# Holding the small products of the head norms behind a turning of attention weights

## The chip, the core and the metric

The kernel runs on one core of one Trainium2 chip. It is one launch that takes all inputs from the chip's memory and writes the whole result back. The metric is the device time of that launch in microseconds (us). TensorE (PE in the profile) multiplies matrices and writes into PSUM, eight banks of 128 partitions by 512 float32 values. VectorE (DVE) and ScalarE (ACT) read those banks. GpSimd (POOL) and SyncE (SP) only issue transfers during the stretch that matters here. Each engine works through a queue of its own in a fixed order, and an instruction at the head of a queue that waits for another engine holds everything behind it.

## The reference

The reference is a trunk of two layers over 512 tokens of width 1024: attention with its output projection, a gated feed-forward part, a short convolution, and another feed-forward part, each with a residual sum and a norm. Only the attention layer is touched. It has 16 heads of 64 values. Eight of them are forgetting heads (softmax with a decay), eight are stick-breaking heads. Queries and keys are normed per head before their products are taken:

```python
q_fox = rms_norm(q[:, :H_FOX], fox_q_g)
k_fox = rms_norm(k[:, :H_FOX], fox_k_g)
q_sb = rms_norm(q[:, H_FOX:], sb_q_g)
k_sb = rms_norm(k[:, H_FOX:], sb_k_g)
...
logits = jnp.einsum('bhqd,bhkd->bhqk', qi, k)
...
return jnp.einsum('bhqk,bhkd->bhqd', w, v)
```

For the stick-breaking heads the weights `w` come from two sigmoids and a running product over the keys; for the forgetting heads they are a softmax. Both are causal, in blocks of 128 queries.

## The kernel before, in words

The heads are worked off in eight pairs, p0 to p7; p0 to p3 are forgetting heads, p4 to p7 stick-breaking heads. Every large product is made of three products of split halves (hi times hi, lo times hi, hi times lo), which are lines L313, L314 and L315 for queries, keys and the output projection (512 columns each) and L570 to L572 for values (256 columns). This text calls them products and value products.

A pair passes through these steps:

- `queries_keys(p)` makes the query and key products into PSUM banks and squares them (`sq`).
- `sums` (L607) sums the squares of each head with eight small products into a bank with the tag "c". ACT copies them out as `flat`, and L615 turns `flat` back with two transposes into the same bank. DVE then computes the reciprocal roots and spreads them over `qwide`.
- `rows` (L640) turns `qwide` with four transposes into a bank of tag "c". DVE multiplies it with the kept queries or keys to `qn` (L642), ACT splits off `qk_hi` (L415), and DVE `qk_lo` (L416). A stick-breaking pair needs this for one of the two operands, a forgetting pair for both.
- `logits(p, u)` (L688) multiplies queries by keys for the unit u of the pair: unit 0 holds query blocks 0 and 1, unit 1 block 2, unit 2 block 3. ACT and DVE make the weights `w` of it. For stick-breaking heads these are the sigmoids (L726, L727), the running product (L729, a scan on DVE) and a product (L732).
- `turn(p, b, w)` turns the weights of block b with transposes into banks of tag "c" (L748 for blocks 0 and 1, L760 for blocks 2 and 3, one bank per head). ACT copies the hi half out (L763), and DVE takes the lo half (L764). Only then is the bank free again.
- `weigh(p)` (L784) multiplies the turned weights by the values; `split` (L415, L416) and the output projection follow.

There are only two banks of tag "c". Sums, the turned `flat`, rows and turnings all pass through them in turn.

The order of the work is made when the kernel is built. A model clock (`clock`) is advanced by `spend(us)` for each piece of work. `after(us, fn)` puts a function on a list that `spend` calls once the clock has passed the given time. `fill(us)` takes products from the list of fillers (query and key products, value products, the first half of the output projection) between the attention steps. `sums` is called `SUMS` = 3.0 model us after the second product of its pair, L615 `FLAT` = 1.5 after that, and `rows` `ROWS` = 8.0 after the scales. The framework then places the instructions into the queues and adds the semaphore waits. The lines that set the times are these:

```python
SUMS, FLAT, ROWS = 3.0, 1.5, 8.0
...
    after(ROWS, lambda: rows(wides))
...
after(SUMS, sums)
...
spend(0.22 * (b + 1))          # the end of turn(p, b, w)
```

Of the kernel before, what the change touches and what calls it, by code (L numbers as in the profile page):

```python
# [42 lines left out]
NORM0 = 4.6  # L43
ORDER = (1, 0, 1, 1, 1, 1, 3)
SUMS, FLAT, ROWS = 3.0, 1.5, 8.0
NSUMS, NROWS, LATE = 4.0, 3.0, 7.0
FILL1, FILL2, BEFORE = 1.5, 3.3, 2.0
UNITS = (0, 1), (2,), (3,)
# [7 lines left out]
def trunk(  # L56
# [20 lines left out]
    def bank(tag):  # L77
        n_ps[0] += 1
        return ps.tile([P, S], F32, tag=tag, name=f"ps{tag}{n_ps[0]}", bufs={"a": 2, "b": 4, "c": 2}[tag])

    def f32(ap):
        return ap.bitcast(F32)
# [130 lines left out]
    clock, later, fillers, quota = [0.0], [], [], [0.0]  # L213

    def spend(us):
        clock[0] += us
        while later and later[0][0] <= clock[0]:
            later.pop(0)[2]()

    def after(us, fn):  # L220
        later.append((clock[0] + us, len(later), fn))
        later.sort(key=lambda e: e[0])

    def flush():
        while later:
            later.pop(0)[2]()

    def fill(us):
        quota[0] += us
        while quota[0] > 0 and fillers:  # L230
            before = clock[0]
            if next(fillers[0], None) is None:
                fillers.pop(0)
            quota[0] -= clock[0] - before
# [71 lines left out]
    def weights(ahead=AHEAD):  # L306
        fetch(1 + ahead)
        at[0] += 1
        return ready[at[0] - 1]
# [84 lines left out]
    def rsqrt(dst, v, n, name):  # L394

        def t(tag, dt=F32):
            return tiny.tile([P, n], dt, tag=f"{tag}{n}", name=f"{tag}_{name}", bufs=2)
        half = t("rh")
        dve.tensor_scalar(half, v, -0.5, None, op0=ALU.mult)
        shifted = t("rs", I32)  # L400
        dve.tensor_scalar(shifted, v.bitcast(I32), 1, None, op0=ALU.logical_shift_right)
        guess = t("rg", I32)
        dve.tensor_scalar(guess, shifted, -1, 0x5F3759DF, op0=ALU.mult, op1=ALU.add)
        y = guess.bitcast(F32)
        for i in range(3):
            a = t("ra")
            dve.tensor_tensor(a, y, y, op=ALU.mult)
            b = t("rb")
            dve.tensor_tensor(b, a, half, op=ALU.mult)
            z = dst if i == 2 else t("ry")  # L410
            dve.scalar_tensor_tensor(z, b, 1.5, y, op0=ALU.add, op1=ALU.mult)
            y = z

    def split(hi, lo, src):
        act.activation(hi, src, AF.Copy)  # L415
        dve.tensor_tensor(lo, src, f32(hi), op=ALU.subtract)  # L416
# [59 lines left out]
    def products(acc, w, order=tuple(range(ND))):  # L476
        for k in order:
            yield mm3(acc, (w[0][:, k, :], w[1][:, k, :]), hs(k), k == order[0], k == order[-1])
# [109 lines left out]
    def queries_keys(p):  # L588


        fox = p < 4
        v = tiny.tile([P, 2, NB, 2], F32, tag="qv", name=f"qv{p}")
        r = tiny.tile([P, 2, NB, 2], F32, tag="qr", name=f"qr{p}")
        kept, got, sqs = {}, {}, []
        halves[p] = got

        def pair(i):
            got[i] = [aw.tile([P, S], F32R, tag=f"qk_{n}{i}", name=f"qk_{n}{p}{i}", bufs=2) for n in ("hi", "lo")]
            return got[i]

        def sums():


            t = bank("c")
            for i in range(2):
                for b in range(NB):
                    pe.matmul(t[32 * b:32 * (b + 1), i * P:(i + 1) * P], head_ones, sqs[i][:, b * P:(b + 1) * P], start=True, stop=True)  # L607
            spend(0.6)
            flat = own.tile([P, S], F32, tag="nrow", name=f"flat{p}", bufs=1)[:, 0:2 * P]
            act.activation(flat, t[:, 0:2 * P], AF.Copy)  # L610
            after(FLAT, lambda: turned_sums(t, flat))

        def turned_sums(t, flat):
            for i in range(2):
                pe.transpose(t[:, (2 + i) * P:(3 + i) * P], flat[:, i * P:(i + 1) * P], ident)  # L615
            spend(0.25)
            dve.scalar_tensor_tensor(
                v.rearrange("p i b h -> p (i b) h"), t[:, 2 * P:4 * P].rearrange("p (j c) -> p j c", c=32)[:, :, 0:2],
                1.0 / HD, least[:, :, None].to_broadcast([P, 2 * NB, 2]), op0=ALU.mult, op1=ALU.add,
            )  # L620
            scales()

        def scales():
            vf, rf = (t.rearrange("p i b h -> p (i b h)") for t in (v, r))
            rsqrt(rf, vf, 16, f"qk{p}")
            if not fox:
                s = q_scale[p] = aw.tile([P, 2, NB, 2], F32, tag="qscale", name=f"qscale{p}", bufs=3)
                dve.tensor_copy(s[:, 0], r[:, 1])
                dve.tensor_scalar(s[:, 1], r[:, 1], -1.0, None, op0=ALU.mult)
            wides = {}  # L630
            for i in kept:
                wides[i] = work.tile([P, S], F32, tag="u0", name=f"qwide{p}{i}").rearrange("p (b h d) -> p b h d", b=NB, h=2)
                dve.tensor_copy(wides[i], r[:, i][:, :, :, None].to_broadcast([P, NB, 2, HD]))
            after(ROWS, lambda: rows(wides))

        def rows(wides):
            for i in kept:
                t = bank("c")
                for b in range(NB):
                    pe.transpose(t[:, b * P:(b + 1) * P], wides[i][:, b].rearrange("p h d -> p (h d)"), ident)  # L640
                n = work.tile([P, S], F32, tag="y", name=f"qn{p}{i}")
                dve.tensor_tensor(n, kept[i], t, op=ALU.mult)  # L642
                split(*pair(i), n)
            done.add(("qk", p))

        for i in range(2):
            acc = bank("b" if p >= 1 else "a")
            yield from products(acc, weights())
            sq = own.tile([P, S], F32, tag="sq", name=f"sq_{p}{i}")
            act.activation(sq, acc, AF.Square)  # L650
            g = head_gains[:, (0 if fox else 2) + (1 - i):][:, 0:1]
            if i == 1 and not fox:
                hi, lo = pair(i)
                act.activation(hi, acc, AF.Copy, scale=g)
                dve.scalar_tensor_tensor(lo, acc, g, f32(hi), op0=ALU.mult, op1=ALU.subtract)
            else:
                kept[i] = work.tile([P, S], F32, tag="u1", name=f"qk{p}{i}", bufs=3)
                act.activation(kept[i], acc, AF.Copy, scale=g)
            sqs.append(sq)
        after(SUMS, sums)  # L660

    def at_once(u):

# [73 lines left out]
    def turn(p, b, w):  # L737


        n = (b + 1) * P  # L740
        if b == 0:
            pts[p] = [aw.tile([P, 20, P], F32R, tag=f"pt{i}", name=f"pt{p}{i}", bufs=1) for i in range(2)]
        if b < 2:
            t = bank("c")
            for e in range(2):
                for k in range(b + 1):
                    c = (e * (b + 1) + k) * P
                    pe.transpose(t[:, c:c + P], w[:, e, k * P:(k + 1) * P], ident)  # L748
            src = t[:, 0:2 * n].rearrange("p (e n) -> p e n", e=2)
            if b:  # L750
                hi, lo = (t_[:, 4:20, :].rearrange("p (e k) q -> p e (k q)", e=2)[:, :, P:3 * P] for t_ in pts[p])
            else:
                hi, lo = (t_[:, 0:20:19, :] for t_ in pts[p])
            act.activation(hi, src, AF.Copy)
            dve.tensor_tensor(lo, src, f32(hi), op=ALU.subtract)
        else:
            for e in range(2):
                t = bank("c")
                for k in range(b + 1):
                    pe.transpose(t[:, k * P:(k + 1) * P], w[:, e, k * P:(k + 1) * P], ident)  # L760
                to = (5 * b, 19 - 6 * b)[e]
                hi, lo = (t_[:, to:to + b + 1, :].rearrange("p k q -> p (k q)") for t_ in pts[p])
                act.activation(hi, t[:, 0:n], AF.Copy)  # L763
                dve.tensor_tensor(lo, t[:, 0:n], f32(hi), op=ALU.subtract)  # L764
        spend(0.22 * (b + 1))

    def weigh(p):
# [77 lines left out]
    rows = {}  # L845
# [34 lines left out]
    load_heads()  # L880
    heads_bank = bank("a")
    qk0 = queries_keys(0)
    part, nk = halve.pop(0)

# [63 lines left out]
    for g in range(len(units) + 2):  # L948
# [8 lines left out]
        if g >= 2 and units[g - 2][1] == len(UNITS) - 1:  # L957
            p = units[g - 2][0]
# [58 lines left out]
    class Blocks:  # L1017

        SUMS = (0, 2), (2, 4), (4, 6), (6, HEAD), (HEAD, 8), (8, 10), (10, HF)
# [670 lines left out]
```

## Time and profile before

| what | us |
|---|---|
| median of 3 runs | 1127.98 (1127.93 to 1128.21) |
| the profiled execution | 1127.62 |
| its span, from the first to the last instruction | 1125.3 |
| PE busy in the span | 1115.6 (99%) |
| DVE busy | 943.4 (84%) |
| ACT busy | 679.9 (60%) |
| the pairs p4 to p7, with the change in them | about 124 to 265 of the span |

The profile's page gives busy time per engine, and the chain that ended last: the path that is followed back from the last instruction through whatever released each step. The waits view lists, per engine and line, which instruction was waited for, with the sum, the count and the longest in us. The timeline lists single instructions: start, duration, engine, line, operation, output and inputs, and in brackets the idle time ahead of it with the instruction that released it. Matmuls overlap in the array, so a row's duration is longer than its step to the next row; the step is what counts. A row "x8" groups eight instructions of one form. The windows view gives, for a stretch of the span, its length and the busy time of each engine, then the granted clock of PE (1.00 is full speed), the DMA share and GB/s.

### The profile page before, as it was taken

The page shows a single profiled execution, that of the slowest core. Times are in us where ns is not written, and L with a number is a line of the kernel's source. Part 1 is how long each engine was busy: PE and PEld are TensorE (multiplying, and loading weights), DVE is VectorE, ACT ScalarE, POOL GpSimd, SP SyncE. Part 2 cuts the span into 40 slices and gives each one's busy share as a digit, 9 for nine tenths or more (in the row PEclk, how much of TensorE's full clock was granted, in tenths as well). Part 3 has the DMA queues.
Part 4 walks back from the last instruction along what each step waited for, and adds up shares of the span by engine and source line. Part 5 has one row for each costly group of instructions (what it writes and reads, how often), then busy time and mean ns, then how long its engine had stood idle before and what let it go on. Part 6 is the DMA issues. An engine that isn't in the chain of part 4 may idle for free.

```text
span 1125.3 us, 19407 instructions
## 1 busy us (share of the span) xinstructions
PE 1115.6 (99%) x7691; PEld 1009.8 (90%) x7691; DVE 943.4 (84%) x1439; ACT 679.9 (60%) x1013; POOL 158.6 (14%) x191
## 2 busy tenths in 40 slices
PE   9999999999999999999999999999999999999998
PEld 7888787878899999999999899988889999998886
DVE  6787888887899787888989889875799888898886
ACT  7556676655466766666557455543456766677553
POOL 4011111111101110014400001111111110014300
PEclk9999999999999999999999999999999999999999
DMA  6678777687877777799963455798887766699951
GB/s 194 173 180 200 179 180 200 155 205 206 197 208 201 208 192 197 206 277 205 228 173 77 120 153 125 157 229 216 207 208 188 177 174 159 183 265 195 233 153 57
DMA packets 175690, 209.34 MB, mean 186 GB/s; under 512 B 7564, under 2 KB 140220, under 8 KB 175600
## 3 DMA queue, kind: packets, MB, share of 16 engines
q0 software_dynamic: 41024, 86.95, 39.1%
q1 hardware_dynamic: 134416, 121.09, 34.8%
q8 instruction: 60, 0.98, 0.4%
q14 instruction: 30, 0.25, 0.1%
q10 hardware_dynamic: 160, 0.07, 0.0%
HBM read 203.10 MB, written 49.28 MB: 224 GB/s over the span
## 4 chain that ended last, share of the span: by engine, by line
PE 90%; DVE 4%; issue 2%; DMA 2%; ACT 1%; SPq 0%; DVEq 0%; ACTq 0%; POOLq 0%
PE psb L1056 25%; PE psb L1602 11%; PE psa L1056 10%; PE psa L1602 8%; PE psb L313 5%; PE psb L315 5%; PE psb L314 5%; PE psa L315 3%; PE psa L313 3%; PE psa L314 3%; PE psa L784 2%; PE psb L688 2%; DMA Xc<-in_conv_w_in 2%; PE psb L570 1%; PE psc L315 1%
## 5 line engine op out<-in xcount | busy, mean ns | idle before, releaser
L292 ACT ACTIVATE whi<-raw 128x1024 fp32r<-128x1024 f32 (+2 forms) x89 | 91.7, 1031 | 93.6 <-PE psb L314 29.9
L293 DVE TENSOR_TENSOR wlo<-raw,whi 128x1024 fp32r<-128x1024 f32 (+2 forms) x89 | 105.5, 1185 | 24.2 <-ACT whi L292 23.2
L1056 PE MATMUL psb<-p_lo,whi_p 128*128 128x256 f32 x432 | 121.7, 282 | 0.0
L1056 PE MATMUL psb<-p_hi,wlo_p 128*128 128x256 f32 x432 | 121.6, 281 | 0.0
L1056 PE MATMUL psb<-p_hi,whi_p 128*128 128x256 f32 x432 | 121.4, 281 | 0.0
L313 PE MATMUL psb<-hs_a,whi 128*128 128x512 f32 x224 | 92.2, 412 | 0.0
L315 PE MATMUL psb<-hs_a,wlo 128*128 128x512 f32 x224 | 88.7, 396 | 0.0
L1056 PEld LDWEIGHTS psb<-p_hi,whi_p 128*128 128x128 f32 x432 | 81.9, 190 | 0.0
L1056 PEld LDWEIGHTS psb<-p_lo,whi_p 128*128 128x128 f32 x432 | 81.4, 188 | 0.0
L1056 PE MATMUL psa<-p_hi,wlo_p 128*128 128x256 f32 x288 | 81.2, 282 | 0.0
L1056 PEld LDWEIGHTS psb<-p_hi,wlo_p 128*128 128x128 f32 x432 | 81.2, 188 | 0.0
L1056 PE MATMUL psb<-q_lo,whi_q 128*128 128x256 f32 x288 | 81.1, 282 | 0.0
L1056 PE MATMUL psa<-p_lo,whi_p 128*128 128x256 f32 x288 | 81.1, 282 | 0.0
L1056 PE MATMUL psb<-q_hi,wlo_q 128*128 128x256 f32 x288 | 81.1, 281 | 0.0
L1056 PE MATMUL psa<-p_hi,whi_p 128*128 128x256 f32 x288 | 80.9, 281 | 0.0
L1056 PE MATMUL psb<-q_hi,whi_q 128*128 128x256 f32 x288 | 80.9, 281 | 0.0
L1602 PE MATMUL psb<-act,whi 128*128 128x256 f32 x352 | 63.2, 282 | 0.0
L423 DVE SCALAR_TENSOR_TENSOR uv<-yv,taps,uv 128x511 f32<-128x511 f32 (+1 forms) x80 | 56.6, 744 | 0.0
L1602 PE MATMUL psb<-whi,act 128*128 128x512 f32 x176 | 56.4, 398 | 0.0
L423 DVE SCALAR_TENSOR_TENSOR ug<-yg,taps,ug 128x511 f32<-128x511 f32 (+1 forms) x80 | 55.5, 744 | 0.0
L1056 PEld LDWEIGHTS psa<-p_hi,whi_p 128*128 128x128 f32 x288 | 54.5, 189 | 0.1
L1056 PEld LDWEIGHTS psb<-q_hi,whi_q 128*128 128x128 f32 x288 | 54.6, 189 | 0.0
(478 smaller groups left out, 3619.3 us busy)
## 6 DMA issues: line engine op xcount, KB each, us to landing
t<-in_ffn_w_up POOLq DMA_DIRECT2D x42, 768.0 KB, 8.0
t<-t POOLq DMA_DIRECT2D x18, 768.0 KB, 5.5
raw<-in_attn_w_in SPq DMA_DIRECT2D x24, 512.0 KB, 5.3
X<-in_ffn_w_up SPq DMA_DIRECT2D x18, 512.0 KB, 5.1
Y<-t SPq DMA_DIRECT2D x18, 512.0 KB, 6.6
three<-t SPq DMA_DIRECT2D x18, 512.0 KB, 3.7
W<-in_ffn_w_up SPq DMA_DIRECT2D x18, 512.0 KB, 4.0
X<-in_ffn_w_up POOLq DMA_DIRECT2D x18, 512.0 KB, 8.0
```

Source lines behind the costliest of these rows:

```text
L292: return (act.activation(hi[:, at_], raw[:, at_], AF.Copy), dve.tensor_tensor(lo[:, at_], raw[:, at_], f32(hi[:, at_]), op=ALU.subtract))
L293: dve.tensor_tensor(lo[:, at_], raw[:, at_], f32(hi[:, at_]), op=ALU.subtract))
L313: made = [pe.matmul(acc, w[0], rhs[0], start=first, stop=False), pe.matmul(acc, w[0], rhs[1], start=False, stop=False), pe.matmul(acc, w[1 ...
L314: pe.matmul(acc, w[0], rhs[1], start=False, stop=False),
L315: pe.matmul(acc, w[1], rhs[0], start=False, stop=last)]
L423: dve.scalar_tensor_tensor(dst[:, d:], src[:, 0:S - d], tap(j), dst[:, d:], op0=ALU.mult, op1=ALU.add)
L570: pe.matmul(acc, lhs[0], w[0], start=first, stop=False)
L688: pe.matmul(ss[e][:, c:c + wide], ql[rows, b * P:n], kl[rows, 0:wide], start=first and b == bs[0], stop=last and b == bs[-1])
L784: pe.matmul(out_, w, t[:, first:first + step * (NB - k - 1) + 1:step, :], start=k == 0 and i == 0, stop=k == NB - 1 and i == 1)
L1056: pe.matmul(to, w[a][:, k, c], x[b][:, k, :], start=fresh and i + k + t == 0, stop=i == 1 and k == 3 and t == 2, skip_group_check=not fresh)
L1602: pe.matmul(to, l, r, start=begin and o + t == 0, stop=end and t == 2 and o == (0 if layer else 1), skip_group_check=not fresh)
```

## The change

`turn` writes down the model time at which a turning of block 2 or 3 ends, and whether the pair is a forgetting one (index 0) or a stick-breaking one (index 1). `sums` and `rows` go through a new function `clear`: if less than `CLEAR` has passed since the end of the last such turning (2.3 model us for a forgetting pair, 4.5 for a stick-breaking one), the call is put on the list again for the time that is left, and `fill` goes on with its products; otherwise it is made at once. No instruction is added or taken away on any engine.

```diff
+CLEAR = 2.3, 4.5
...
+    turned = [-1e9, 0]
+
+    def clear(fn):
+
+        wait = turned[0] + CLEAR[turned[1]] - clock[0]
+        if wait > 0:
+            after(wait, lambda: clear(fn))
+        else:
+            fn()
...
-            after(ROWS, lambda: rows(wides))
+            after(ROWS, lambda: clear(lambda: rows(wides)))
...
-        after(SUMS, sums)
+        after(SUMS, lambda: clear(sums))
...
+        turned[:] = clock[0] + 0.22 * (b + 1), p >= 4
         spend(0.22 * (b + 1))
```

Behind the new lines the line numbers grow, by 11 in the functions of the pairs and by 12 from `turn` on: L607, L615, L640, L642, L688, L760 and L764 of before are L618, L626, L651, L653, L699, L771 and L775 of the changed kernel, L784 is L796, L830 is L842, and the products L313 to L315 and L570 to L572 are L324 to L326 and L581 to L583.

The queues of POOL and SP are the same in both kernels. Those of PE, ACT and DVE differ only from p4's sums to the end of the attention layer. The three places where most moves follow.

The first is PE's queue after the turning of p5's block 2 (psc_2577 and psc_2583 are its two banks, one for each head), with p6's rows (L640 into psc_2601). Before:

```order
L760 MATMUL psc_2577<-ident,w_2429 128x128 x3
L760 MATMUL psc_2583<-ident,w_2429 128x128 x3
L313 MATMUL psb_2564<-hs_a_119,whi_2325 128x512
...
L315 MATMUL psb_2564<-hs_a_119,wlo_2326 128x512
L640 MATMUL psc_2601<-ident,qwide_2512 128x128 x4
L313 MATMUL psb_2564<-hs_a_119,whi_2325 128x512
...
L760 MATMUL psc_2671<-ident,w_2551 128x128 x2
L688 MATMUL psb_2615<-qk_hi_2608,qk_hi_2403 128x256
```

Between the turning and the rows stand twelve products; six more follow, and then the turning of p5's block 3 and p6's first logits.

The second is PE's queue further on, with the sums of p7 (L607 into psc_2697); between the end of the turning of p5's block 3 and them stand 22 value products, the last of which is the first row. Before:

```order
L570 MATMUL psb_2713<-whi_2410,hs_a_119 128x256
L607 MATMUL psc_2697<-sq_2560,head_ones 32x128 x4
L607 MATMUL psc_2697<-sq_2648,head_ones 32x128 x4
L571 MATMUL psb_2713<-wlo_2411,hs_a_119 128x256
L572 MATMUL psb_2713<-whi_2410,hs_a_119 128x256
L688 MATMUL psb_2723<-qk_hi_2608,qk_hi_2403 128x384
L688 MATMUL psb_2724<-qk_hi_2608,qk_hi_2403 128x384
L615 MATMUL psc_2697<-ident,flat_2706 128x128 x2
L688 MATMUL psb_2723<-qk_lo_2609,qk_hi_2403 128x384
```

In the changed kernel both places have become one (psc_2583 and psc_2589 are here the banks of p5's block 2, psc_2639 that of p6's rows, psc_2686 that of p7's sums, psc_2697 the first one of p5's block 3):

```order
L771 MATMUL psc_2583<-ident,w_2435 128x128 x3
L771 MATMUL psc_2589<-ident,w_2435 128x128 x3
...
L326 MATMUL psb_2546<-hs_a_119,wlo_2315 128x512
L581 MATMUL psb_2620<-whi_2410,hs_a_119 128x256
...
L651 MATMUL psc_2639<-ident,qwide_2515 128x128 x4
L581 MATMUL psb_2620<-whi_2547,hs_a_119 128x256
...
L618 MATMUL psc_2686<-sq_2542,head_ones 32x128 x4
L618 MATMUL psc_2686<-sq_2607,head_ones 32x128 x4
L771 MATMUL psc_2697<-ident,w_2565 128x128 x4
L699 MATMUL psb_2650<-qk_hi_2646,qk_hi_2403 128x256
```

p6's rows now stand behind twelve products and eighteen value products; behind them come six value products, p7's sums, the first half of the turning of p5's block 3 and then p6's first logits. The second half of that turning, and the transposes of `flat` (L626) for p7, stand behind those logits.

The third place is DVE's queue around the `qn` of p7's rows (L642 before, L653 after). Before:

```order
L564 SCALAR_TENSOR_TENSOR v_2660<-psb_2820,ncol_n_332,v_2660 128x4x64
L642 TENSOR_TENSOR qn_2865<-qk_2562,psc_2860 128x512
L416 TENSOR_TENSOR qk_lo_2868<-qn_2865,qk_hi_2867 128x512
L729 SCALAR_TENSOR_TENSOR rest<-rest,begin 128x512
L732 TENSOR_TENSOR w_2877<-w_2877,rest 128x512
```

After:

```order
L304 TENSOR_TENSOR wlo_2905<-raw_2906,whi_2904 128x1024
L740 SCALAR_TENSOR_TENSOR rest<-rest,begin 128x512 x2
...
L775 TENSOR_TENSOR pt_2833<-psc_2926,pt_2832 128x384
L842 TENSOR_TENSOR h<-psa_2910,h 128x512
L731 MEMSET rest 128x2
L842 TENSOR_TENSOR h<-psa_2936,h 128x512
L304 TENSOR_TENSOR wlo_2951<-raw_2952,whi_2950 128x1024
L653 TENSOR_TENSOR qn_2968<-qk_2544,psc_2963 128x512
L842 TENSOR_TENSOR h<-psa_2956,h 128x512
L427 TENSOR_TENSOR qk_lo_2971<-qn_2968,qk_hi_2970 128x512
```

The multiplication for p7's rows has moved from ahead of the scans of p6's block 3 to behind them, and behind the lo halves of the turning of p6's block 2 (L775), two residual sums (L842) and a split of weights (L304). On PE, the logits of p6's block 3, 33 products of one or the other kind and a turning stood between p7's rows and its first logits before; now six products and three transposes do.

## The prediction

> **What bounds the kernel now.** I read the page first, then the waits of PE, then windows over the stretches where the change moves instructions, and last the timeline around each wait.
>
> ```profile
> PE 1115.6 (99%) x7691; PEld 1009.8 (90%) x7691; DVE 943.4 (84%) x1439; ACT 679.9 (60%) x1013; POOL 158.6 (14%) x191
> PE 90%; DVE 4%; issue 2%; DMA 2%; ACT 1%; SPq 0%; DVEq 0%; ACTq 0%; POOLq 0%
> ...
> PE psc L640 <- DVE pt L764: 1.3, 1, 1.3
> PE psc L607 <- DVE pt L764: 1.1, 2, 0.7
> PE psa L784 <- DVE o L791: 0.5, 1, 0.5
> ...
> 192.00:197.00 5.00, 3.68 (x20) 2.78 (x19) 4.59 (x7) 2.10 (x5) 0.71 (x1) 1.00 0.81 193
> 195.00:220.00 25.00, 23.03 (x187) 20.20 (x187) 21.23 (x49) 15.31 (x33) 3.52 (x5) 1.00 0.61 147
> 265.00:300.00 35.00, 35.00 (x159) 28.51 (x158) 30.08 (x52) 20.17 (x29) 3.86 (x5) 1.00 0.84 200
> ```
>
> PE carries the time: it is busy for 99% of the span and holds 90% of the chain. All its matmuls remain, so the change can only win back time in which PE waits. The waits view (sum, count, longest) shows where that is: small products into "c" banks wait for DVE's lo half of a turning (L764), once ahead of p6's rows and twice ahead of sums. The windows (length, busy time of PE, weight loads, DVE, ACT and POOL, then the clock) show PE idle for 1.32 us in 192 to 197, with DVE busy for 4.59 of the 5 us. From 265 to 300 PE never stops, and no engine's order differs there, so I expect what is won or lost before 265 to stand at the end.
>
> **What the holding removes.** The three waits, with the rows around them:
>
> ```profile
> 126.44 0.48 PE L313 MATMUL psb<-hs_a,whi 128*128 128x512 f32 x1
> ...
> 127.44 0.40 PE L314 MATMUL psb<-hs_a,whi 128*128 128x512 f32 x1
> 127.67 0.40 PE L315 MATMUL psb<-hs_a,wlo 128*128 128x512 f32 x1
> 128.51 0.64 PE L607 MATMUL psc<-sq,head_ones 128*32 128x128 f32 x16 [0.44 <-DVE pt L764]
> 129.09 0.50 PE L313 MATMUL psb<-hs_a,whi 128*128 128x512 f32 x1
> ...
> 192.00 0.48 PE L313 MATMUL psb<-hs_a,whi 128*128 128x512 f32 x1
> ...
> 194.66 0.40 PE L315 MATMUL psb<-hs_a,wlo 128*128 128x512 f32 x1
> 196.38 0.66 PE L640 MATMUL psc<-ident,qwide 128*128 128x128 f32 x4 [1.32 <-DVE pt L764]
> 196.79 0.48 PE L313 MATMUL psb<-hs_a,whi 128*128 128x512 f32 x1
> ...
> 204.05 0.28 PE L572 MATMUL psb<-whi,hs_a 128*128 128x256 f32 x1
> 204.16 0.28 PE L570 MATMUL psb<-whi,hs_a 128*128 128x256 f32 x1
> 205.10 0.65 PE L607 MATMUL psc<-sq,head_ones 128*32 128x128 f32 x16 [0.66 <-DVE pt L764]
> 205.67 0.38 PE L571 MATMUL psb<-wlo,hs_a 128*128 128x256 f32 x1
> ...
> 127.77 0.69 DVE L764 TENSOR_TENSOR pt<-psc,pt 128x512 fp32r<-128x512 f32 x1
> ...
> 195.77 1.01 DVE L764 TENSOR_TENSOR pt<-psc,pt 128x384 fp32r<-128x384 f32 x2
> ...
> 204.36 1.28 DVE L764 TENSOR_TENSOR pt<-psc,pt 128x512 fp32r<-128x512 f32 x2
> ```
>
> The step from one product to the next is 0.23 us (127.44 to 127.67), from one value product to the next 0.11 (204.05 to 204.16). A product ahead of sums needs about 0.1 more for the change of form; that is my reading of the bracket, which is 0.40 less than the step of 0.84 at 127.67. So the waits are worth 0.84 - 0.33 = 0.51 us (p4's sums), 1.72 - 0.23 = 1.49 (p6's rows) and 0.94 - 0.21 = 0.73 (p7's sums): 2.73 together.
>
> Does the holding clear them? For p4's sums, twelve products instead of six stand ahead, so they are reached at 126.44 + 12 x 0.23 = 129.2; the first lo half ended at 127.77 + 0.69 = 128.46. Clear by 0.7 us. p6's rows now stand behind twelve products and eighteen value products: 192.00 + 2.8 + 18 x 0.12 = 197.0. The pair of lo halves ended at 196.78, and the rows need only the first of them (some 0.5 earlier). Clear. p7's sums follow 1.1 us after, when the second lo half has ended too. Clear. I take the full 2.73. The bounds are 1.32 (the bracket of L640 alone) and 2.73: more than was waited for can't be won here.
>
> [...] This trace has 0.23 us per product, so I go by the row.
>
> **What moving costs.** The small blocks themselves cost the same wherever they stand: L640's four transposes take 0.41 us from 196.38 to 196.79, the sums 0.58 from 128.51 to 129.09. Three things are new.
>
> ```profile
> 197.07 0.69 DVE L642 TENSOR_TENSOR qn<-qk,psc 128x512 f32<-128x512 f32 x1 [0.28 <-PE psc L640]
> 197.79 0.63 ACT L415 ACTIVATE qk_hi<-qn 128x512 fp32r<-128x512 f32 x1 [3.69 <-DVE qn L642]
> 198.46 0.69 DVE L416 TENSOR_TENSOR qk_lo<-qn,qk_hi 128x512 fp32r<-128x512 f32 x1 [0.70 <-ACT qk_hi L415]
> ...
> 198.58 0.50 PE L688 MATMUL psb<-qk_hi,qk_hi 64*128 64x256 f32 x4
> 199.01 0.39 PE L570 MATMUL psb<-whi,hs_a 128*128 128x256 f32 x1
> 199.33 0.50 PE L688 MATMUL psb<-qk_lo,qk_hi 64*128 64x256 f32 x4
> ```
>
> (1) p6's rows stand closer to p6's logits. From the start of L640 to the end of `qk_hi` it takes 198.42 - 196.38 = 2.04 us, to the end of `qk_lo` 199.15 - 196.38 = 2.77. After the change the rows (0.41), six value products (0.7), p7's sums (0.58) and four transposes (0.44) stand ahead of the logits: 2.13. So `qk_hi` comes in time by 0.1 if DVE is free for `qn`. `qk_lo` is needed after the first third of the logits (0.43) and two value products (0.32 + 0.11), at 2.99, and comes in time by 0.2. But the sums of p7 now hold one of the two "c" banks until their `flat` is turned back (L626, behind the logits). The two halves of the turning of p5's block 3 must share the other one: the second waits for `qn`'s successors, ACT's copy and DVE's lo half of the first (0.69 by the row at 127.77). An ACT copy of that shape takes 0.63 (the row at 197.79), so the first is free some 1.3 us after its transposes. To fill that PE has the logits and two value products, 3 x 0.43 + 0.43 = 1.7, if DVE, which has `qk_lo` to make in between (0.69), is not late. I book 0.4 for this place and 0.1 for a similar one at p5's rows; the bounds are 0 and 1.3 (copy and lo half wholly uncovered).
>
> (2) p7's rows. Of before:
>
> ```profile
> 215.61 0.60 PE L640 MATMUL psc<-ident,qwide 128*128 128x128 f32 x4
> ...
> 223.16 0.51 PE L688 MATMUL psb<-qk_hi,qk_hi 64*128 64x256 f32 x4
> ...
> 218.35 1.22 DVE L729 TENSOR_TENSOR_SCAN rest<-rest,begin 128x512 f32<-128x512 f32 x1
> 219.67 0.69 DVE L732 TENSOR_TENSOR w<-w,rest 128x512 f32<-128x512 f32 x1
> ...
> 223.15 1.21 DVE L293 TENSOR_TENSOR wlo<-raw,whi 128x1024 fp32r<-128x1024 f32 x1
> ...
> 225.82 0.68 DVE L830 TENSOR_TENSOR h<-psa,h 128x512 f32<-128x512 f32 x1
> ```
>
> They had 223.16 - 215.61 = 7.55 us before their logits and waited for nothing. Now they have 0.41 + 6 x 0.23 + 0.33 = 2.1, against the 2.04 that `qn` and `qk_hi` need if DVE takes `qn` at once. Ahead of `qn` DVE has, since the logits of p6's block 3, two scans and two products (2 x 1.32 + 2 x 0.61 = 3.9 us by these rows), two lo halves (1.0), two residual sums (1.2) and a split of weights (1.2): 7.3 us. On PE 24 products (5.6) and six transposes (0.7), then six more products (1.4) stand over the same stretch: 7.7 us. Both begin with those logits, since the scans wait for them. So DVE arrives within a few tenths of PE, and the queue in front of `qn` is the thinnest margin of the change. The first residual sum there (L842) frees a bank for the third output group; it stands behind the scans and the lo halves, and PE reaches that group at about the time when it ends. I book 0.6 there, between 0 and the 1.2 of one scan or split more in front.
>
> (3) Breaking a group of logits costs: the value product at 199.01 takes 0.32 to the next row instead of 0.12. One such break is added at p7's logits: 0.2, between 0 and 0.4.
>
> The tail of attention has waits too:
>
> ```profile
> 232.77 0.40 PE L315 MATMUL psa<-o_hi,wlo 128*128 128x512 f32 x1
> 233.33 1.46 PE L784 MATMUL psa<-pt,v 128*128 128x512 f32 x8 [0.16 <-DVE h L830]
> ...
> 236.03 0.40 PE L315 MATMUL psa<-o_hi,wlo 128*128 128x512 f32 x1
> 236.89 1.49 PE L784 MATMUL psa<-pt,v 128*128 128x512 f32 x8 [0.45 <-DVE o L791]
> ```
>
> They are 0.56 - 0.23 = 0.33 and 0.86 - 0.23 = 0.63. The changed queues still put a residual sum or a sum of heads ahead of either L796, so I book them as they are; bounds 0.9 less, 1.0 more.
>
> Sum: -2.73 + 0.5 + 0.6 + 0.2 = -1.43. The profiled execution took 1127.62 us, its span and 2.3 us around it that nothing here changes, so its like would take 1126.2. It lies 0.36 below the median of 1127.98; on the median's footing I say 1126.5.
>
> **The rivals.**
>
> All of the waits go and nothing takes their place: 1127.98 - 2.73 = 1125.25. For it: by (1) and (2) every chain could just be in time. Against it: DVE is busy for 21.23 of 25 us from 195 to 220; the same work has to fit into less.
>
> Slower, by one mechanism: p7's `qn` comes late because of DVE's queue. Each further scan or split that stands ahead of it costs 1.2 us, and with `qk_lo` behind a residual sum another 0.7. The time passes that of before when PE waits there for more than 1.43 + 0.6 = 2.0 us; two such instructions and the late `qk_lo` (3.1) give 1128.0 - 2.0 + 3.1 = 1129.1, and as much again if the turning behind it comes late too. The thin margin in (2) speaks for it; that DVE's and PE's sums differ by less than one scan speaks against.
>
> Nothing changes in effect: the three waits come back at the next user of the same two banks, 1127.5 to 1128.0. For it: the "c" banks and DVE have the same work. Against it: the waits view has only these three for "c" banks in the stretch, though many more small blocks pass through them.
>
> A clock that drops: the granted clock is 1.00 in the window with 1.32 us idle, so waits did not touch it. Were p6's stretch from 192 to 197 at half clock, its 3.68 us of PE work would take 3.7 more: 1130.2. [...]
>
> **How the numbers follow.** A chance of 0.50 for the forecast (own range 1125.6 to 1127.4), 0.20 for the waits that go without a substitute, 0.14 for no effect, 0.14 for the late `qn`, 0.02 for the clock. A measurement of this kernel tells about 0.2%, 2.3 us, from no change: faster means below 1125.7, slower above 1130.2. Faster gets 0.20 from the first rival and 0.04 from the forecast's low edge; slower 0.09 from the late `qn` where it costs the turning too, and 0.01 from the clock, whose 1130.2 is the boundary; the rest is the same. The range reaches from below the first rival, 1124.9, to the late `qn` at 1129.1, and leaves out the gravest of it and the clock.
>
> **What would show it.** Right: no wait on L775 ahead of L618 or L651, the window from the turning at p6 fully busy, a small wait at the second half of the turning of p5's block 3, and some tenths at L699 or L324 by p7's rows. Wrong: PE waiting for `qk_hi`, `qk_lo` or a residual sum for over 2 us between p7's rows and the last L796; or the waits of L618 and L651 still there; or PE idle after 265.

## The result and the profile after

The changed kernel takes 1126.24 us (median of 14 runs), the kernel before 1128.04 us on the same chip (median of 14). The ratio is 0.9983, with a 95% interval from 0.9975 to 0.9990: 1.9 us less, between 1.1 and 2.8. The profiled execution took 1126.22 us. The prediction said 1126.5, with the same (within 0.2%) as the likeliest sign.

The page and PE's waits of the changed kernel (engine, line, what it waited for; sum, count, longest in us), and windows over three stretches:

```profile
span 1123.9 us, 19405 instructions
PE 1115.5 (99%) x7691; PEld 1010.2 (90%) x7691; DVE 943.1 (84%) x1439; ACT 679.6 (60%) x1013; POOL 157.5 (14%) x191
...
PE psa L324 <- DVE rest L731: 1.1, 1, 1.1
...
PE psa L796 <- DVE h L842: 0.9, 1, 0.9
...
192.00:197.00 5.00, 5.00 (x29) 4.21 (x28) 4.90 (x10) 2.96 (x6) 0.89 (x1) 1.00 0.82 191
220.00:245.00 25.00, 23.00 (x123) 17.57 (x122) 21.43 (x35) 12.77 (x25) 2.96 (x5) 1.00 0.78 201
265.00:300.00 35.00, 35.00 (x159) 28.54 (x158) 30.70 (x54) 20.88 (x31) 3.85 (x5) 1.00 0.83 210
```

The second of these windows, of before:

```profile
220.00:245.00 25.00, 24.38 (x132) 18.76 (x131) 22.80 (x36) 16.50 (x33) 2.37 (x3) 1.00 0.85 213
```

No small product waits for a lo half (L775) any more. The stretch from 192 to 197 is full, and from 220 to 245 PE now lacks 2.0 us, against 0.6 before. The two waits that cause this are for residual sums: the row that names L731 is one of them, since the memset stands between the two sums of that row's place in DVE's queue.

The profiles of the kernels here also differ where all of them have the same order: by up to 1.8 us in what lies ahead of 100 us (the first product of all starts at 6.88 us before, at 7.35 in the changed kernel), and by up to 2.7 us behind 285. What the change does is read more sharply from the stretch between, from one product ahead of p4's sums to one after attention, the same two in every kernel. Its first 26 us, where the order is also the same, repeat within 0.02 us:

```profile
100.24 0.48 PE L313 MATMUL psb<-hs_a,whi 128*128 128x512 f32 x1
...
285.09 0.48 PE L313 MATMUL psb<-hs_a,whi 128*128 128x512 f32 x1
```

```profile
100.77 0.48 PE L324 MATMUL psb<-hs_a,whi 128*128 128x512 f32 x1
...
284.10 0.48 PE L324 MATMUL psb<-hs_a,whi 128*128 128x512 f32 x1
```

Before (the first fence) it is 285.09 - 100.24 = 184.85 us, after 284.10 - 100.77 = 183.33: 1.52 us less. "The stretch" below is always this one. The places of the three old waits, in the timeline of the changed kernel:

```profile
126.97 0.48 PE L324 MATMUL psb<-hs_a,whi 128*128 128x512 f32 x1
...
129.59 0.40 PE L326 MATMUL psb<-hs_a,wlo 128*128 128x512 f32 x1
129.92 0.64 PE L618 MATMUL psc<-sq,head_ones 128*32 128x128 f32 x16
130.49 0.45 PE L699 MATMUL psb<-qk_hi,qk_hi 64*128 64x384 f32 x2
...
198.37 0.28 PE L583 MATMUL psb<-whi,hs_b 128*128 128x256 f32 x1
198.49 0.60 PE L651 MATMUL psc<-ident,qwide 128*128 128x128 f32 x4
...
199.53 0.28 PE L583 MATMUL psb<-whi,hs_b 128*128 128x256 f32 x1
199.74 0.65 PE L618 MATMUL psc<-sq,head_ones 128*32 128x128 f32 x16
200.31 0.66 PE L771 MATMUL psc<-ident,w 128*128 128x128 f32 x4
200.90 0.51 PE L699 MATMUL psb<-qk_hi,qk_hi 64*128 64x256 f32 x4
...
202.45 0.66 PE L771 MATMUL psc<-ident,w 128*128 128x128 f32 x4
...
201.63 0.69 DVE L775 TENSOR_TENSOR pt<-psc,pt 128x512 fp32r<-128x512 f32 x1
```

The steps into the small blocks are 0.33, 0.12 and 0.21 us, without idle time: 0.51, 1.49 and 0.73 us of waiting are gone. And the places where PE waits now, on PE and then on DVE:

```profile
215.61 0.50 PE L699 MATMUL psb<-qk_hi,qk_hi 64*128 64x512 f32 x2
...
222.63 0.39 PE L326 MATMUL psa<-o_hi,wlo 128*128 128x512 f32 x1
224.09 0.47 PE L324 MATMUL psa<-o_hi,whi 128*128 128x512 f32 x1 [1.08 <-DVE rest L731]
...
225.56 0.60 PE L651 MATMUL psc<-ident,qwide 128*128 128x128 f32 x4
...
227.81 0.50 PE L699 MATMUL psb<-qk_hi,qk_hi 64*128 64x256 f32 x4
...
228.76 0.48 PE L324 MATMUL psa<-o_hi,whi 128*128 128x512 f32 x1
229.18 0.51 PE L699 MATMUL psb<-qk_lo,qk_hi 64*128 64x256 f32 x4
...
236.20 1.39 PE L796 MATMUL psa<-pt,v 128*128 128x512 f32 x8
238.51 1.46 PE L796 MATMUL psa<-pt,v 128*128 128x512 f32 x8 [0.93 <-DVE h L842]
...
217.76 1.22 DVE L304 TENSOR_TENSOR wlo<-raw,whi 128x1024 fp32r<-128x1024 f32 x1
218.89 2.33 DVE L740 TENSOR_TENSOR_SCAN rest<-rest,begin 128x512 f32<-128x512 f32 x2
221.15 1.27 DVE L743 TENSOR_TENSOR w<-w,rest 128x512 f32<-128x512 f32 x2
222.33 1.01 DVE L775 TENSOR_TENSOR pt<-psc,pt 128x384 fp32r<-128x384 f32 x2
223.26 1.29 DVE L842 TENSOR_TENSOR h<-psa,h 128x512 f32<-128x512 f32 x2
...
226.20 0.69 DVE L653 TENSOR_TENSOR qn<-qk,psc 128x512 f32<-128x512 f32 x1 [0.51 <-PE psc L651]
```

The third group of the output projection starts 1.46 - 0.23 = 1.23 us late: its bank is freed by the first of the two residual sums at 223.26, which stands behind scans, products and lo halves on DVE. The scans themselves start only at 218.89, 3.28 us after the logits that they depend on (215.61): ACT and DVE have splits of weights ahead of them, on DVE the row at 217.76. `qn` of p7 is not late; DVE itself waited 0.51 us for p7's rows. But PE had lost its 1.23 us ahead of those rows: had it come to them that much earlier, DVE would not have been free before 224.47 + 1.22 = 225.69 (the split of weights behind the residual sums), and `qn` would have come late by some 0.8 us, by an estimate from these rows. The second half of the weighing of p6 starts 1.09 us late (the step inside the L796 block is 1.20 instead of 0.11), where before its two halves had waited 0.33 and 0.63.

### The profile page after: what moved, and what is told of

Its sections match the earlier page's. It is cut to its first block, busy times and chain, and to the rows that moved or that the text cites. A ratio compares the mean times of both kernels' runs of the same rounds, so it can differ in the third digit from the quotient of the medians.

```text
span 1123.9 us, 19405 instructions
## 1 busy us (share of the span) xinstructions
PE 1115.5 (99%) x7691; PEld 1010.2 (90%) x7691; DVE 943.1 (84%) x1439; ACT 679.6 (60%) x1013; POOL 157.5 (14%) x191
## 4 chain that ended last, share of the span: by engine, by line
PE 91%; DVE 3%; issue 2%; DMA 2%; ACT 1%; DVEq 0%; ACTq 0%; POOLq 0%
PE psb L1068 25%; PE psb L1614 11%; PE psa L1068 10%; PE psa L1614 8%; PE psb L324 6%; PE psb L325 6%; PE psb L326 6%; PE psa L326 2%; PE psa L324 2%; PE psa L325 2%; PE psb L699 2%; DMA Xc<-in_conv_w_in 2%; PE psa L796 1%; PE psc L771 1%; PE psc L326 1%
## 5 line engine op out<-in xcount | busy, mean ns | idle before, releaser
L304 DVE TENSOR_TENSOR wlo<-raw,whi 128x1024 fp32r<-128x1024 f32 (+2 forms) x89 | 105.6, 1187 | 25.7 <-ACT whi L303 24.9
L324 PE MATMUL psb<-hs_a,whi 128*128 128x512 f32 x224 | 92.0, 411 | 0.0
L326 PE MATMUL psb<-hs_a,wlo 128*128 128x512 f32 x224 | 88.7, 396 | 0.0
L1614 PEld LDWEIGHTS psb<-act,whi 128*128 128x128 f32 x352 | 54.2, 189 | 0.5 <-DVE act L1018 0.3
```

Of the source, the lines that this page charges most:

```text
L304: dve.tensor_tensor(lo[:, at_], raw[:, at_], f32(hi[:, at_]), op=ALU.subtract))
L324: made = [pe.matmul(acc, w[0], rhs[0], start=first, stop=False), pe.matmul(acc, w[0], rhs[1], start=False, stop=False), pe.matmul(acc, w[1 ...
L326: pe.matmul(acc, w[1], rhs[0], start=False, stop=last)]
L1614: pe.matmul(to, l, r, start=begin and o + t == 0, stop=end and t == 2 and o == (0 if layer else 1), skip_group_check=not fresh)
```

## The experiments

Each kernel was timed beside the kernel before on the same chip; the ratio is always to that. The chips were not the same for all rows, so the medians of two rows should not be compared, but their ratios. The stretch is from the one profiled execution of each.

| kernel | median us | ratio to before (95%) | stretch us, against before's 184.85 |
|---|---|---|---|
| the changed kernel | 1126.24 | 0.9983 (0.9975 to 0.9990) | -1.52 |
| sums_only | 1129.04 | 1.0002 (0.9993 to 1.0011) | +0.81 |
| rows_only | 1126.76 | 0.9983 (0.9975 to 0.9992) | -0.96 |
| fox_only | 1127.24 | 0.9989 (0.9980 to 0.9998) | -0.80 |
| only_p6_rows | 1127.42 | 0.9996 (0.9982 to 1.0011) | -1.18 |
| free_p7_rows | 1125.43 | 0.9976 (0.9966 to 0.9986) | -1.87 |
| copied_dve | 1125.67 | 0.9968 (0.9956 to 0.9981) | -2.84 |
| before_copied | 1127.92 | 0.9994 (0.9986 to 1.0003) | +0.11 |
| free_copied_dve | 1125.78 | 0.9967 (0.9955 to 0.9978) | -2.41 |
| copied_pool | 1159.86 | 1.0258 (1.0235 to 1.0281) | +26.62 |
| stick_40 | 1127.26 | 0.9987 (0.9978 to 0.9995) | +0.31 |
| stick_40_copied | 1127.28 | 0.9987 (0.9978 to 0.9996) | +0.16 |
| dve_load | 1128.13 | 0.9997 (0.9989 to 1.0006) | -0.49 |

The theory: the gain is the sum of waits for "c" banks that go, less waits that the moved blocks bring on. Its first rival: any new dealing of the filling products would have gained as much.

**The change in halves.** sums_only keeps the holding for sums, rows_only for rows.

```diff
-            after(ROWS, lambda: clear(lambda: rows(wides)))
+            after(ROWS, lambda: rows(wides))        # sums_only
...
-        after(SUMS, lambda: clear(sums))
+        after(SUMS, sums)                           # rows_only
```

> Only sums go through the holding; rows are put as before. Theory A: p4's sums (0.51) and p7's sums (0.73) wait no more, p6's rows wait 1.3 to 1.5 us again behind twelve products; time 1.2 below before less whatever the moved p7 rows cost (0 to 0.6): 1126.8 to 1127.4. Rival C (the gain comes from dealing out the fillers anew, not from these waits): the same gain as the whole change, 1126.2, with the wait at p6's rows in place.

> Only rows go through the holding; sums are put as before. Theory A: p6's rows wait no more (1.49 gained), p4's sums wait 0.5 again, p7's sums now stand directly behind the second half of a turning and the logits and wait 0.4 to 1.2, and p7's rows bring the wait of about 1 us at a residual sum; 0.0 to 0.8 below before: 1127.2 to 1128.0. Rival C: as the whole change, 1126.2.

The waits of sums_only, and the second place of the first row in its timeline:

```profile
PE psc L651 <- DVE pt L775: 2.5, 2, 1.3
PE psa L796 <- DVE h L842: 1.2, 1, 1.2
...
220.05 0.40 PE L325 MATMUL psa<-o_lo,whi 128*128 128x512 f32 x1
221.66 0.66 PE L651 MATMUL psc<-ident,qwide 128*128 128x128 f32 x4 [1.22 <-DVE pt L775]
```

As expected p6's rows wait again. What I had put at 0 to 0.6 was 1.4 us: with p7's sums later and its rows not held, the rows come only six value products and eight products behind a turning, and wait for its lo half as p6's do. PE's idle time at p6's weighing grew too, from 0.6 to 1.2 us, which I had not booked. Sums alone gain nothing. rows_only did better than I expected, by its ratio (0.9983) and by 0.2 us in the stretch: p4's wait is there (0.51), p6's and p7's are gone, and p7's sums, directly behind p6's logits, have none of the 0.4 to 1.2 that I had put there. The first rival falls: the same fillers dealt out anew without clearing p6's wait gave no gain.

**One place at a time.** fox_only sets the second number of `CLEAR` to 0. only_p6_rows holds a single call of the kernel before.

```diff
-CLEAR = 2.3, 4.5
+CLEAR = 2.3, 0.0                                    # fox_only
...
-            after(ROWS, lambda: clear(lambda: rows(wides)))
+            after(ROWS, lambda: clear(lambda: rows(wides)) if p == 6 else rows(wides))
-        after(SUMS, lambda: clear(sums))
+        after(SUMS, sums)                           # only_p6_rows, both
```

> Only the holding behind forgetting pairs, 2.3, is kept; behind stick-breaking pairs nothing is held. That moves p4's sums and rows and p5's sums a little; all behind is as before. Theory A: p4's wait goes, 0.5 below before, 1127.5 to 1128 on a footing of 1128.2; p6's wait of 1.3 and p7's of 0.7 stay. Rival C: nothing, or more than 1 us.

> The kernel before with one call held: p6's rows. Theory A (each wait for a 'c' bank is a term of its own): p4's wait of 0.5 stays, p6's 1.5 goes, p7's sums come directly behind p6's logits and wait 0.2 to 0.6 instead of 0.7, p7's rows stay where they hurt nothing; 1.4 to 2.0 below before, ratio 0.9982 to 0.9988: this one call would bring most of what the whole change does. Rival C (anew dealt fillers): no more than 0.5 below before.

In fox_only the p4 part gains 0.80: the 0.51 of the wait, and 0.29 in many small steps. PE does not pass less often between products and small blocks there (22 times instead of 20 in the part that is in another order). What differs most is which block follows which: the last transpose of `flat` or of rows takes 0.20 us to the next row where logits follow, and 0.03 to 0.11 where products, a weighing or a turning follow (the two of `flat`, with a step of 0.11 between them: 0.31 us to the logits from 130.59 of before, 0.22 to a turning from 150.93, and 0.14 to a weighing from 132.95 of the changed kernel). Of the four such places in this part two stand directly ahead of logits before, and none in fox_only. That 0.29 I had booked at nothing. only_p6_rows gains 1.18 in the stretch, less than the 1.4 to 2.0 expected; its interval by the runs includes 1, no change at all. It clears p6's 1.49 and p7's 0.73, and about 1 us comes back in pieces of 0.1 to 0.3, the largest of them at the transposes of p5's turning and at a residual sum. The two add up: -0.80 - 1.18 = -1.98, and the change without p7's rows, next, has -1.87.

**p7's rows.**

```diff
-            after(ROWS, lambda: clear(lambda: rows(wides)))
+            after(ROWS, lambda: rows(wides) if p == 7 else clear(lambda: rows(wides)))
```

> p7's rows are not held, all else as in the changed kernel; they go back among p5's value products, and p7's first logits come between the second and the third group of the output projection. Theory A (the waits for 'c' banks make the gain, and p7's held rows bring the new wait of 1.1 us of L324 for a residual sum behind DVE's scans): the three waits of before stay away, the logits give DVE 1.0 us more before the third group starts, and the wait falls to 0.0 to 0.4; about 0.8 us below the changed kernel, near 1125.4. Rival B (the wait belongs to the group of products, wherever the rows stand, since the residual sum stands behind the same scans and lo halves): 0.8 to 1.2 us of wait stay at the third group, time as the changed kernel, 1126.2.

```profile
PE psc L759 <- DVE pt L766: 0.7, 1, 0.7
...
PE psa L324 <- DVE rest L731: 0.4, 1, 0.4
PE psa L796 <- DVE h L842: 0.3, 1, 0.3
PE psa L796 <- DVE o L803: 0.3, 1, 0.3
```

Of its waits, the one at the third group fell from 1.1 to 0.4, as theory A said, and the weighing's as well; in their place 0.7 us came at the transposes of p6's first turning (L759), with p7's rows among the value products ahead. The stretch is 0.35 shorter than the changed kernel's, so by the stretch holding p7's rows costs about a fifth of what the rest of the change gains. The intervals of the two ratios overlap.

**The bank of the output groups.** copied_dve lets ScalarE copy each finished group of the first half of the output projection out of its bank; DVE adds from the copy. before_copied has the same in the kernel before, free_copied_dve in free_p7_rows, and in copied_pool GpSimd adds.

```diff
+    def residual_copied(o, acc):
+        t = own.tile([P, S], F32, tag="sq", name=f"part{o}")
+        act.activation(t, acc, AF.Copy)
+        dve.tensor_tensor(h[:, o, :], t, h[:, o, :], op=ALU.add)    # copied_pool: nc.gpsimd
...
-                fillers.append(output(0, residual))
+                fillers.append(output(0, residual_copied))
```

> The changed kernel, but in the first half of the output projection ScalarE copies each finished group out of its bank and DVE adds from the copy, so that the bank does not wait for DVE's queue. Theory A: the waits of 1.1 us (third group) and 0.9 us (second half of the weighing of p6) for a residual sum go; a wait of 0.2 to 0.5 for qk_hi at p7's first logits takes part of it back; 1.3 to 1.9 us below the changed kernel, 1124.3 to 1124.9. Rival D (DVE's work of this stretch is the bound, the bank only where it shows): PE waits for as much at the next place that needs DVE, p7's logits or the turning, and the time stays within 0.4 us of 1126.2.

> The kernel before, with ScalarE's copy of each finished group of the first half of the output projection, as in copied_dve; PE's order is that of before. Theory A: the waits of the two halves of p6's weighing (0.33 and 0.63) go in part, 0.3 to 0.9 below before, and p4's, p6's and p7's waits for 'c' banks stay. So the copy's gain in copied_dve over the changed kernel (waits of 1.1 and 0.9) would mostly be what the change had brought on. Rival D (the copies give DVE slack everywhere): 1.3 or more below before here too.

> free_p7_rows and copied_dve in one. Theory A: of the waits that free_p7_rows had left, 0.4 and 0.3 for residual sums go, 0.7 at the transposes of p6's first turning for DVE and 0.3 at the weighing stay; 0.4 to 0.8 below free_p7_rows, ratio to before 0.9964 to 0.9972. Rival D (DVE's work is the bound by now): no further gain over either, ratio 0.9968 to 0.9978.

In copied_dve both waits for residual sums are gone and one of 1.06 us has come (a step of 1.22, of which two transposes take 0.16), in its timeline at

```profile
237.40 0.41 PE L759 MATMUL psc<-ident,w 128*128 128x128 f32 x2
238.62 0.50 PE L324 MATMUL psa<-o_hi,whi 128*128 128x512 f32 x1 [0.81 <-DVE o L803]
```

where the next group needs the bank of the weighing, which DVE's sum of heads frees. The stretch is 1.32 us shorter than the changed kernel's, as theory A had it. The wait for `qk_hi` that theory A set against the gain did not come: the framework moved PE's order there, and p7's logits stand behind the whole turning and two products. In before_copied, where I had expected 0.3 to 0.9, there is nothing to gain: the waits of 0.33 and 0.63 merge into one of 1.13 for the same DVE sum. So the copies take back what the change had brought on, and no more. free_copied_dve gains 0.54 on free_p7_rows, in theory A's range, but is not better than copied_dve (182.44 against 182.01 us in the stretch, the ratios level): with the copies, taking p7's rows out of the holding brings nothing more. Both lie below the changed kernel in their ratios, with intervals that overlap its own.

> As copied_dve, but GpSimd adds the copy to the residual instead of VectorE, which takes eight sums of 0.68 us out of DVE's queue. Theory A (what is left of PE's waits at the end of attention, 1.06 us in copied_dve for the sum of p6's heads on DVE, is DVE's queue): that wait falls to 0 to 0.5; the stretch from 100 to 285 us is 0.3 to 1.0 shorter than the 182.0 of copied_dve; ratio to before 0.9955 to 0.9968. Rival E (GpSimd's sums slow DVE or the transfers that GpSimd issues, or come late themselves): the stretch stays at 182 or grows.

Rival E, and far beyond it. The waits and a row of the groups on GpSimd:

```profile
PE psa L324 <- ACT part L846: 23.3, 1, 23.3
...
ACT part L846 <- POOL h L847: 27.6, 1, 27.6
POOL t L105 <- DMA t<-in_ffn_w_up: 128.3, 18, 9.3
...
L847 POOL TENSOR_TENSOR h<-part,h 128x512 f32<-128x512 f32 x8 | 13.2, 1733 | 17.1 <-ACT part L846 17.1
```

GpSimd needs 1.73 us for a sum, but that is not what costs. Its queue waits for transfers up to 9.3 us at a time before it issues the next (between 231 and 254, within PE's wait, it is busy for 4.47 of 23 us); the sums stand behind such waits, the copies wait for the sums' tiles, and PE for the copies.

**How near the edges are.** dve_load computes p7's `qn` three times over. stick_40 holds for 4.0 instead of 4.5; stick_40_copied adds the copies.

```diff
-                dve.tensor_tensor(n, kept[i], t, op=ALU.mult)
+                for _ in range(3 if p == 7 else 1):
+                    dve.tensor_tensor(n, kept[i], t, op=ALU.mult)
...
-CLEAR = 2.3, 4.5
+CLEAR = 2.3, 4.0
```

> The changed kernel with p7's qn computed three times over, 1.2 us more of DVE ahead of qk_hi; the framework answers by setting seven more products (1.6 us) ahead of p7's logits, which no longer have the turning's second half before them. Theory A (the margin of qn at p7 is about 0.3 us in the changed kernel; what comes later costs one for one unless products fill it): PE waits 0 to 0.4 at the logits, and 0 to 1 us more at the weighing of p6, which comes closer; 0 to 1.2 above the changed kernel. Rival B (DVE has slack here): as the changed kernel within 0.2 in the stretch, 183.3.

> The changed kernel with 4.0 for 4.5. p6's rows then stand behind twelve products and fifteen value products, p7's sums behind nine more; p7's rows stand behind the first nine products after the logits of p6's block 3, one bank ahead of its turning, and p7's logits behind 24 products. Theory A: p6's rows are reached at 192.0 + 2.8 + 1.8 = 196.6 on the clock of before and the first lo half ends at 196.3: no wait; p7's third group starts behind the logits as in free_p7_rows; the stretch is 182.5 to 183.3 (free_p7_rows 182.98, changed kernel 183.33). Rival F (p7's rows ahead of the turning hold one of the two banks and the turning's second half waits for qn behind the scans): 0.7 to 1.3 of wait at L771, the stretch 183.6 or more.

> stick_40 with the copies of copied_dve. Theory A: the waits for residual sums that stick_40 has go, 0.4 to 1.0 off its stretch; ratio to before 0.9960 to 0.9970. Rival D: no gain over stick_40.

dve_load takes 1.03 us more in the stretch than the changed kernel, in theory A's range; the seven products in front of p7's logits hide the late `qn`, and PE waits 1.59 us at the weighing of p6 instead of 0.93. stick_40 is rival F, with a wait of 1.8 where it said 0.7 to 1.3. Its timeline and windows (length, busy PE, weight loads, DVE, ACT, POOL, then the granted clock):

```profile
220.62 0.40 PE L324 MATMUL psa<-o_hi,whi 128*128 128x512 f32 x1
222.84 0.55 PE L771 MATMUL psc<-ident,w 128*128 128x128 f32 x3 [1.82 <-DVE qn L653]
...
224.73 0.63 PE L324 MATMUL psa<-o_hi,whi 128*128 128x512 f32 x1
225.15 0.63 PE L325 MATMUL psa<-o_lo,whi 128*128 128x512 f32 x1
...
222.00:224.00 2.00, 1.16 (x7) 1.03 (x8) 2.00 (x5) 1.09 (x2) 0.21 (x1) 0.99 0.85 134
224.00:226.00 2.00, 2.00 (x6) 1.20 (x4) 0.93 (x3) 0.18 (x1) 0.00 (x0) 0.50 1.00 187
226.00:228.00 2.00, 2.00 (x15) 1.68 (x15) 1.75 (x2) 1.11 (x2) 0.00 (x0) 0.65 1.06 323
```

p7's rows stand directly ahead of the first half of p6's turning there, the second half waits for the bank that `qn` reads, and `qn` stands behind DVE's scans: a step of 2.22 us. And behind it the granted clock is 0.50 (224 to 226). The copies do not touch that bank, and stick_40_copied shows the same wait of 1.8 us and gains next to nothing over stick_40 in median and stretch, as rival D said. Both have longer stretches than before and yet ratios of 0.9987: the profiled execution of stick_40 lost some 1.7 us to the clock, by the estimate in the last section, and its mean clock of 0.998, which is also that of the profiled execution of stick_40_copied, is not that of all executions.

## Why the prediction was right, point by point

- The three waits that go: booked at 2.73 us, all three gone in the trace at the rows shown. The counts of products ahead of each were enough. The step of 0.23 us per product held: twelve products took 129.92 - 126.97 = 2.95 us with the change of form.
- p6's rows close to their logits, with one bank for both halves of a turning: booked at 0.5, measured at nothing. The logits at 200.90 and the turnings beside them have no idle time; DVE's lo half of the first half of the turning ends at 201.63 + 0.69 = 202.32, 0.13 us before the second half starts. That step was too dear.
- p7's rows: booked at 0.6 (0 to 1.2), measured 1.23, just above the upper end. The mechanism is the one written down (the first residual sum behind scans and lo halves, and the third group's bank). What I had wrong is the start: "Both begin with those logits" holds for PE, but DVE's scans began 3.28 us after them, with splits of weights ahead that I had not counted, so the residual sum was late by the whole 1.23 us, where I had PE reach that group "at about the time when it ends". The part that I had called the thinnest margin, `qn` itself, cost nothing, because PE had already been held up by the residual sum: DVE waited for the rows there. With 1.2 us more of it (dve_load) PE still has no wait at the logits, though the stretch pays 1.03 elsewhere.
- The tail of attention: booked as unchanged at 0.96, measured 1.09.
- The extra break of p7's logits: booked at 0.2; the product at 228.76 takes 229.18 - 228.76 = 0.42 instead of 0.23, so 0.19. Against it stand small steps that I had put at nothing ("The small blocks themselves cost the same wherever they stand"): with the blocks in other places they gave 0.29 in p4's part alone, in fox_only.

So -2.73 + 1.23 + 0.13 = -1.37 from the waits, and -0.15 from small steps in sum, the break among them, make the -1.52 that the stretch shows; the prediction had -1.43. The nearness is partly luck: the 0.5 at p6 and the 0.6 at p7 were both wrong by as much, in opposite directions.

Of the rivals, "all waits go" is what copied_dve comes close to (-2.84), with another engine's help. "Nothing changes" is refuted by the rows. The slower rival asked for a late `qn`; stick_40 is where it happens, at 4.0 instead of 4.5, and in its profile the 1.82 us come with a granted clock of 0.50, and I had given a clock that drops 2 chances in 100.

## What to carry to other kernels

Where a bound engine waits for a buffer, the count of independent work items ahead of the wait times their step tells whether a move clears it, and it is worth doing place by place: here p4's part and p6's rows held the whole gain, and one held call too many gave, by the stretch, a fifth of it back. After such a move look for the next buffer whose release stands behind long work on another engine's queue, and count that engine's work from where it really starts. A copy by an engine with time to spare (ACT is busy for 60% of the span), which only frees the buffer, was worth nearly as much on top of the change (1.32 us of the stretch) as the change itself (1.52), and nothing without it.

## What the runs showed of the hardware

In the profile of stick_40 the granted clock of PE fell shortly after a single short wait. PE was idle for 1.82 us, at a clock of 1.00 from 220 to 222; about a microsecond after it had gone on at 222.84, the clock was 0.50, and the step of a product went from 0.23 to 0.42 us (224.73 to 225.15). By an estimate from the windows (0.65 from 223.8 to 224.4, 0.50 from there to 227.2, 0.91 from 227.2 to 228.2) it lasted 3.4 us, until about 227.4, which costs half of that, 1.7 us, nearly as much as the wait. The profiled execution of stick_40_copied has the same wait of 1.8 us and the same mean clock, 0.998. Idle times of 1.32 us (before, ahead of p6's rows, 1.00 from 194 to 200) and 1.59 us (dve_load, 1.00 from 234 to 242) left it at 1.00. The mean clock of a profile does not follow its longest wait: in free_copied_dve it is 0.998, and no wait of PE there is longer than 1.3 us; in dve_load, with 1.6 us, it is 0.999. In copied_pool the clock was 0.50 for some 6 us behind the wait of 23 us (0.50 in the windows from 254.4 to 260.6, 0.99 from there to 261.4). That the wait in stick_40 brought the drop on is not shown.

Nor is the mean clock the same in all executions of a kernel. Five of the 11 executions of stick_40, the profiled one among them, have a mean granted clock of 0.998, the other six 0.999 or 1.000; the medians of the two groups are 1127.77 and 1126.72 us. Of stick_40_copied seven of 12 have 0.998, with 1127.89 against 1125.71 us; of dve_load three of 11, and of the kernel before on the same chip one of 29. A drop to half for 3.4 us takes 0.0015 from the mean over the span, which fits 0.998; whether and where the executions without a profile dropped is not shown. The executions with the higher mean put stick_40_copied 1.0 us below stick_40, but they are only five and six. What makes the difference between executions is open.

Left open too: why the medians put rows_only level with the changed kernel while its stretch is 0.56 us longer. Both intervals allow it, and in the two profiles 0.40 of it came back behind 285, where the order is the same.
